# Strassen's seven products for five slabs of an MLP's first matrix product

## The chip, the cores and the metric

The kernel runs on one core of a Trainium2 chip. Its time is that of one execution on the device in microseconds; the figure for a kernel is the median of several runs. A core has a matrix engine (TensorE, "PE" in a profile, with its weight loads as "PEld"), a vector engine (VectorE, "DVE"), a scalar engine (ScalarE, "ACT"), a general engine (GpSimd, "POOL") and one that issues transfers (SyncE, "SP"). Each engine runs its own queue of instructions in order, and they wait for each other by semaphores. SBUF is the on-chip memory with 128 partitions, PSUM the memory in which TensorE sums its products.

## The reference

One layer of an encoder on 512 tokens of 1024 channels. A mixer (attention in a neighbourhood, a state-space branch, gates and an output projection w_o) is followed by a layer norm, then the channel sub-layer, which is what is edited, and a last layer norm:

```python
def sq_relu_mlp(x, w1, w2):
    return jnp.square(jax.nn.relu(x @ w1)) @ w2

h = layer_norm(DN_ALPHA * h + mix, ln1_g[l], ln1_b[l])
h = layer_norm(DN_ALPHA * h + sq_relu_mlp(h, w_ff1[l], w_ff2[l]), ln2_g[l], ln2_b[l])
```

Here x is 512 x 1024, w1 1024 x 4096 and w2 4096 x 1024, all float32.

## The kernel before

A float32 product is made from three products in a reduced-precision float form: each operand is split into a high part (a rounding copy) and a low part (the operand less the high part), and `mm3` (L402 to L406) issues high x high, low x high and high x low. The high part of weights is a copy on ScalarE (L386), the low part a subtraction on VectorE (L387). `split_weights` does both for a slab that SyncE loads (L378, buffer `ws`); the two parts go into rotating buffers (`wh`, `wl`, and a third pair `wh3`, `wl3`).

The first product of the channel sub-layer runs transposed: 32 tiles of 128 columns of w1 (the weights) against 512 tokens, stored as `h1Th` and `h1Tl` (high and low parts of the normalised tokens, channels in partitions). The tiles form four quarters `fq` of eight tiles `f`; two tiles share a slab of 256 columns `s`, 1 MB of weights, so a slab is 2 tiles x 8 blocks of 128 channels x 3 = 48 matmuls of 128 weights columns by 512 tokens. The tiles of the first two slabs of quarter 0 start ahead of the others, in halves of the tokens, before the second half's norm is done. A tile is taken out of PSUM by ScalarE, as a relu (L1672) and a square (L1678) into `r2`.

The second product, w2, uses Strassen's seven products already: `ff2_strassen` is a generator whose every step is one chunk. A chunk takes a block of w2 loaded by GpSimd's transfers (L1554, `w2r`), to which a second block is added by an accumulating transfer (L1565), splits it (L1570, L1571), and for the other operand takes differences of `r2` (L1588) and splits (`sqh`, `sql`). `into` adds the products to `acc`. The blocks rotate over three places, two of their own and one of the slab buffers `ws`. Three chunks are issued before each slab of quarter 2; quarter 3 runs the same way and is then multiplied plainly.

`acc` also holds the layer norm's result, which needs two more passes, times a row and plus a row (the "affine"): eight operations of 128 x 1024 on GpSimd (L1695), issued behind tile 4 of quarter 0. The first three w2 loads are held behind tile 0 of quarter 1 (`begin`).

The program's text gives the order only in part: a scheduler sets each engine's queue when the program is built, from dependencies and estimated durations, and buffers in pools are given out in the order of the text.

Of the kernel before, what the change touches and what calls it, by code (L numbers as in the profile page):

```python
# [19 lines left out]
P = 128  # L20
S = 512
# [336 lines left out]
def encoder_layer(ctx, tc, x, w_in, w_attn_br, w_ssd_br, w_o, w_ff1, w_ff2, pcols, rows64,  # L358
# [44 lines left out]
    def mm3(o, lh, ll, rh, rl, start, stop):  # L403
        nc.tensor.matmul(o, lh, rh, start=start, stop=False)  # L404
        nc.tensor.matmul(o, ll, rh, start=False, stop=False)  # L405
        return nc.tensor.matmul(o, lh, rl, start=False, stop=stop)  # L406
# [47 lines left out]

    def to_channels(xn, t0, nt, gcol, bcol, dsth, dstl, pool, name):

        for k in range(KD):
            tp = psx.tile([P, nt, P], F32, tag="tr", bufs=BANKS["tr"], name=f"tp_{name}_{k}")
            for t in range(nt):
                nc.tensor.transpose(tp[:, t, :], xn[t][:, k * P : (k + 1) * P], ident)  # L460
            v = pool.tile([P, nt * P], F32, tag="tc_v", bufs=2, name=f"tc_{name}_{k}")
            nc.scalar.activation(v, tp, AF.Identity, bias=pc[:, bcol + k : bcol + k + 1],
                                 scale=pc[:, gcol + k : gcol + k + 1])
# [23 lines left out]
    def bank(name, tag, shape):  # L487
        return plan.tile(name, tag, psx, shape, F32)
# [958 lines left out]
    ep = tc.tile_pool(name="ep", bufs=1, reuse_waits="tile")  # L1447
    epp = ep.__enter__()
    wo_pool = tc.tile_pool(name="wo", bufs=1, reuse_waits="tile")
    wop = wo_pool.__enter__()  # L1450
# [27 lines left out]
    for t2 in range(2):  # L1478
# [22 lines left out]
        for t in toks:  # L1501
            layer_norm_core(epp, h0[t], acc[t], f"1_{t}")
        to_channels([acc[t] for t in toks], toks[0], 2, PC_G1, PC_B1, h1Th, h1Tl, epp, f"h1_{t2}")
    wo_pool.__exit__(None, None, None)
    ep.__exit__(None, None, None)
    gp.__exit__(None, None, None)
    rx0.__exit__(None, None, None)


    ffp = ctx.enter_context(tc.tile_pool(name="ffp", bufs=1, reuse_waits="tile"))  # L1510
    NQ = D_FF // D
# [5 lines left out]
    def parts(name, shape):  # L1517

        turn["parts"] += 1
        if turn["parts"] % 3 == 0:  # L1520
            return third(w3p, name, shape)
        return [wide(wp.tile([P, 2112], F32R, tag=n, name=f"{n}_{name}"), shape[1])
                for n in ("wh", "wl")]

    def raw(name):
        turn["raw"] += 1
        pool, tag = ((ffp, "wr"), (ffp, "wr"), (wp, "ws"))[turn["raw"] % 3]
        return pool.tile([P, 4, 512], F32, tag=tag, bufs=2, name=f"w2r_{name}")
# [11 lines left out]
    def ff2_strassen(h, q0, r2):  # L1540
# [100 lines left out]
        def right1(c):  # L1641
# [4 lines left out]
            for i in range(2):  # L1646
# [7 lines left out]
                           (0, 0))  # L1654

    def ff1_tile(fq, f, last):

# [4 lines left out]
        else:  # L1662
# [8 lines left out]
        rl = ffp.tile([P, S], F32, tag="rl", bufs=2, name=f"rl{fq}_{f}")  # L1671
        nc.scalar.activation(rl, ps, AF.Relu)  # L1672
# [9 lines left out]
    def squares(name, dtype=F32):  # L1682
        return ffp.tile([P, KD, S], dtype, tag="r2", bufs=3, name=name)

    r2 = [squares(f"r2_{fq}") for fq in range(2)]
    for fq in range(2):
        for f in range(KD):
            ins = ff1_tile(fq, f, False)
            if fq == 1 and f == 0:
                begin = ins  # L1690
            if fq == 0 and f == 4:

                for t in range(NT):
                    for i, o in ((0, ALU.mult), (1, ALU.add)):
                        aff = nc.gpsimd.tensor_tensor(out=acc[t], in0=acc[t], in1=row1[i], op=o)  # L1695
                        if i == 0:
                            tc.add_manual_dep(aff.ins, ins.ins.name, mybir.DependencyInfo(
                                mybir.DependencyClass.Sync, mybir.DependencyReason.DATA),
                                reason="behind the first channels")

    r2.append(squares("r2_2"))
    run = ff2_strassen(0, 0, r2[:2])
# [17 lines left out]
    rest = ffp.tile([P, 2, 4, 512], F32R, tag="r2", bufs=3, name="w2_4")  # L1720
    slabs = [[split_weights([(w_ff2, r0 + k0 * P, i * 512, 512)], 4, 512, f"f2_3_{i}_{k0}", *x)
              for k0, x in y] for i, y in enumerate((
                  ((0, [ffp.tile([P, 4, 512], F32R, tag="wr", bufs=2, name=f"w2{n}_0") for n in "hl"]),
                   (4, [rest[:, n] for n in range(2)])),
# [85 lines left out]
```

## Time and profile before

| | |
|---|---|
| runs, median (lowest to highest) | 1183.74 us (1183.55 to 1184.21, three runs) |
| profiled execution: its span, the time by which the page's numbers go | 1182.6 us |
| TensorE busy | 1159.1 us, 98% |
| VectorE, ScalarE, GpSimd busy | 757.7, 614.7, 545.2 us |
| ten tiles of the first product (874.0 to 928.4) | 54.4 us, TensorE busy throughout |

The span is that of one execution under the profiler, the runs are timed without it. Windows of the profile are given in microseconds from the span's start. A row of a timeline has the start, the time, the engine, the line of the program, the operation, out<-in, the shape and in brackets the idle time before it with what ended it; a row of groups has minimum, median and maximum of one instruction's time in nanoseconds. The matmul's times overlap, so their cost is read from the distance of starts.

### The profile page before, as it was taken

How to read it: one execution, taken by the hardware profiler on the slowest of the kernel's cores; microseconds unless marked ns; L12 is line 12 of the kernel's file. 1: busy time of each engine (PE TensorE's matmuls, PEld its weight loads, DVE VectorE, ACT ScalarE, POOL GpSimd, SP SyncE). 2: the span in 40 equal slices, each digit the busy share in tenths (PEclk: the TensorE clock that was granted, in tenths of full speed). 3: DMA queues.
4: the chain of work that ended last, by engine and by line, in shares of the span. 5: the costliest groups of instructions: out<-in, count | busy, mean ns of one | idle time of the engine just before them, and what ended most of it. 6: DMA issues, size and time to landing. Idle time of an engine off the chain costs nothing.

```text
span 1182.6 us, 16453 instructions
## 1 busy us (share of the span) xinstructions
PE 1159.1 (98%) x6138; PEld 990.3 (84%) x6138; DVE 757.7 (64%) x1363; ACT 614.7 (52%) x1033; POOL 545.2 (46%) x588
## 2 busy tenths in 40 slices
PE   5999999999999999999999999999999999999997
PEld 5988798989888888888888888888988888878886
DVE  7757475666656656443789975556543658488856
ACT  6676573837354654423667864342253545365410
POOL 1268968777788786304567540016046121222000
PEclk9999999999999999999999999999999999999999
DMA  6353333333333331333333223544236977889511
GB/s 201 97 157 125 102 130 107 112 116 129 102 114 107 126 120 59 107 105 85 87 87 86 56 71 107 166 147 138 85 107 184 237 187 200 192 211 233 160 51 54
DMA packets 129407, 149.19 MB, mean 126 GB/s; under 512 B 22960, under 2 KB 101808, under 8 KB 129328
## 3 DMA queue, kind: packets, MB, share of 16 engines
q1 hardware_dynamic: 115696, 112.63, 31.0%
q0 software_dynamic: 13056, 34.61, 11.9%
q8 instruction: 48, 0.79, 0.3%
q10 hardware_dynamic: 576, 0.92, 0.2%
q14 instruction: 31, 0.25, 0.1%
HBM read 145.90 MB, written 2.23 MB: 125 GB/s over the span
## 4 chain that ended last, share of the span: by engine, by line
PE 86%; DMA 4%; DVE 4%; issue 2%; POOL 2%; ACT 1%; SPq 1%; DVEq 0%; POOLq 0%; ACTq 0%
PE ps_f L406 8%; PE ps_f L404 8%; PE ps_f L405 8%; PE ps_x L406 5%; PE ps_x L404 5%; PE ps_x L405 4%; PE ps_abr L1368 4%; PE ps_z L404 3%; PE ps_z L405 3%; PE ps_z L406 3%; PE ps_sbr L404 2%; PE ps_sbr L406 2%; PE ps_sbr L405 2%; PE yd L977 2%; DMA w2r<-in_w_ff 2%; PE ps_g L405 2%
## 5 line engine op out<-in xcount | busy, mean ns | idle before, releaser
L784 DVE SCALAR_TENSOR_TENSOR cv<-ps_x,pc,cv 128x511 f32<-128x511 f32 (+1 forms) x128 | 95.7, 748 | 25.6 <-ACT cv L776 22.0
L405 PE MATMUL ps_f<-h1Th,wl_f 128*128 128x512 f32 (+1 forms) x288 | 104.0, 365 | 0.0
L404 PE MATMUL ps_f<-h1Th,wh_f 128*128 128x512 f32 (+1 forms) x288 | 103.6, 365 | 0.0
L406 PE MATMUL ps_f<-h1Tl,wh_f 128*128 128x512 f32 (+1 forms) x288 | 102.0, 365 | 0.0
L1571 DVE TENSOR_TENSOR wl_f<-w2r,wh_f 128x1024 fp32r<-128x1024 f32 x42 | 50.0, 1220 | 62.5 <-ACT wh_f L1570 62.2
L404 PE MATMUL ps_z<-wh_z,hTh 128*128 128x256 f32 x256 | 75.2, 294 | 0.6 <-DVE cv L784 0.5
L406 PE MATMUL ps_z<-wl_z,hTh 128*128 128x256 f32 x256 | 71.5, 279 | 0.0
L405 PE MATMUL ps_z<-wh_z,hTl 128*128 128x256 f32 x256 | 71.5, 279 | 0.0
L1565 POOL DMA_DIRECT2D w2r<-in_w_ff x30 | 36.3, 1415 | 75.6 <-DMA w2r<-in_w_ff 49.0
L405 PE MATMUL ps_f<-wh_f,sql 128*128 128x512 f32 x168 | 65.3, 390 | 0.5 <-DVE sql L1571 0.5
L406 PE MATMUL ps_f<-wl_f,sqh 128*128 128x512 f32 x168 | 65.3, 390 | 0.1
L1570 ACT ACTIVATE wh_f<-w2r 128x1024 fp32r<-128x1024 f32 x42 | 42.6, 1052 | 43.1 <-DMA w2r<-in_w_ff 32.8
L404 PE MATMUL ps_f<-wh_f,sqh 128*128 128x512 f32 x168 | 64.9, 389 | 0.0
L1099 DVE TENSOR_TENSOR ysacc<-ps_sbr,ysacc 128x512 f32<-128x512 f32 x56 | 38.6, 690 | 39.9 <-PE ps_sbr L406 39.7
L404 PEld LDWEIGHTS ps_f<-h1Th,wh_f 128*128 128x128 f32 x288 | 53.9, 188 | 9.0 <-ACT rl L1672 0.2
L405 PEld LDWEIGHTS ps_f<-h1Th,wl_f 128*128 128x128 f32 x288 | 53.9, 188 | 8.7
L387 DVE TENSOR_TENSOR wl_f<-ws_f,wh_f 128x1024 fp32r<-128x1024 f32 x36 | 47.2, 1347 | 20.9 <-ACT wh_f L386 20.7
L406 PEld LDWEIGHTS ps_f<-h1Tl,wh_f 128*128 128x128 f32 x288 | 52.8, 188 | 8.7
L404 PE MATMUL ps_x<-hTh,wh_bc 128*128 128x512 f32 (+1 forms) x144 | 56.7, 394 | 0.0
L404 PE MATMUL ps_sbr<-yTh,wh_sbr 128*128 128x512 f32 x128 | 55.6, 434 | 0.7 <-ACT yTh L1076 0.4
L406 PE MATMUL ps_x<-hTl,wh_bc 128*128 128x512 f32 (+1 forms) x144 | 53.4, 371 | 1.7 <-DVE hTl L626 1.7
L404 PE MATMUL ps_x<-hTh,wh_x 128*128 128x512 f32 (+1 forms) x144 | 54.6, 379 | 0.0
(344 smaller groups left out, 3734.2 us busy)
## 6 DMA issues: line engine op xcount, KB each, us to landing
ws_f<-in_w_ff SPq DMA_DIRECT2D x20, 1024.0 KB
w2r<-in_w_ff POOLq DMA_DIRECT2D x18, 1024.0 KB, 7.6
bc<-acs_d SPq DMA_DIRECT2D x32, 512.0 KB
w2r<-in_w_ff POOLq DMA_DIRECT2D x30, 512.0 KB, 8.8
ws_bc<-in_w_in SPq DMA_DIRECT2D x16, 512.0 KB
ws_x<-in_w_in SPq DMA_DIRECT2D x8, 1024.0 KB
ws_z<-in_w_in SPq DMA_DIRECT2D x8, 1024.0 KB
ws_g<-in_w_in SPq DMA_DIRECT2D x8, 1024.0 KB
```

What stands on the lines that cost most here:

```text
L387: (eng[i] if isinstance(eng, tuple) else eng).tensor_tensor(out=lo[:, k], in0=st[:, k], in1=hi[:, k].bitcast(F32), op=ALU.subtract)
L404: nc.tensor.matmul(o, lh, rh, start=start, stop=False)
L405: nc.tensor.matmul(o, ll, rh, start=False, stop=False)
L406: return nc.tensor.matmul(o, lh, rl, start=False, stop=stop)
L784: op("DVE", 0.75, lambda j=j, o=o, n=n: nc.vector.scalar_tensor_tensor(out=acc()[:, o], in0=ps()[:, n], scalar=tap(j), in1=acc()[:, o], op ...
L977: nc.tensor.matmul(yd()[:, c % 2, h * HD : (h + 1) * HD], bc()[:, 1, h, :], xtok()[:, c, h * HD : (h + 1) * HD], start=True, stop=True)
L1099: op("DVE", 0.69, lambda d=d, ps=ps: nc.vector.tensor_tensor(out=ysacc[:, d, :], in0=ps(), in1=ysacc[:, d, :], op=ALU.add), r=[(ps.name, 0 ...
L1368: ins.append(nc.tensor.matmul(pss[j], u, v, start=k + p == 0, stop=k == KD - 1 and p == 2))
L1565: nc.gpsimd.dma_start(t, rows(i, n, c, k), accum_op=ALU.add)
L1570: nc.scalar.activation(hi[:, k], x, AF.Copy)
L1571: low = nc.vector.tensor_tensor(out=lo[:, k], in0=x, in1=hi[:, k].bitcast(F32), op=ALU.subtract)
```

## The change

Five slabs, slab 3 of quarter 0 and the four of quarter 1, are multiplied as a 2 x 2 product of halves: the 1024 channels in two halves of four blocks, and the slab's 256 columns in two tiles of 128; the 512 tokens are halved too. Seven products of (128 columns x 4 blocks x 256 tokens) take the place of eight: 7 x 4 x 3 = 84 matmuls of 256 tokens in place of 48 of 512.

On the token side `to_channels` keeps its float32 values (`h1a`, `h1b`), and the four sums s1 to s4 are made from them once, one on GpSimd and three on VectorE, and split. On the weight side `pair_weights` first splits three of the slab's blocks (pair "a"), then forms four differences in the slab's own buffer, two on VectorE and two on GpSimd, each in place of a block that isn't needed any more, and splits the four blocks again (pair "b"). So a slab takes two of the rotating pairs, and its buffer is held until the last low part of "b". `ff1_pair` issues the seven products into four banks of PSUM; ScalarE takes out `m1` and `m75`, VectorE adds to p26 and p43, GpSimd makes `x75` and the fourth quarter of the tile, and one relu and one square of 128 x 1024 end the slab.

Other edits go with it. The affine moves from GpSimd to VectorE, two operations behind `m75` of each of the first four slabs. `begin` becomes `m75` of slab 0 of quarter 1. The first chunk of w2 is issued ahead of the last slab's products. The buffer of `r2` is divided in two pools, sums and differences share space with buffers that are free by then, and the memory for descriptors of transfers that GpSimd issues becomes 4096 bytes.

```diff
+    s1, s2, s3, s4 = sums = [srp.tile([P, 4, 256], F32, name=f"s{i}") for i in range(4)]
+    nc.gpsimd.tensor_tensor(out=s1, in0=h1b[:, 0:4], in1=h1b[:, 4:8], op=ALU.add)
+    nc.vector.tensor_tensor(out=s3, in0=h1a[0], in1=h1b[:, 0:4], op=ALU.subtract)
+    nc.vector.tensor_tensor(out=s2, in0=s1, in1=h1a[0], op=ALU.subtract)
+    nc.vector.tensor_tensor(out=s4, in0=h1a[1], in1=s2, op=ALU.subtract)
+    for i in (2, 0, 1, 3):
+        nc.scalar.activation(sh[i], sums[i], AF.Copy)
+        nc.vector.tensor_tensor(out=sl[i], in0=sums[i], in1=sh[i].bitcast(F32), op=ALU.subtract)
...
+    def pair_weights(fq, s):
...
+        def both(hi, lo, src):
+            nc.scalar.activation(hi, src, AF.Copy)
+            nc.vector.tensor_tensor(out=lo, in0=src, in1=hi.bitcast(F32), op=ALU.subtract)
...
+        both(ah[:, 0:2], al[:, 0:2], w4[:, :, 0])
+        both(ah[:, 2], al[:, 2], b22)
+        diff(nc.vector, b11, b12, b11)
+        diff(nc.gpsimd, b12, b22, b12)
+        diff(nc.vector, b22, b22, b11)
+        diff(nc.gpsimd, b21, b21, b22)
+        both(bh[:, 0:2], bl[:, 0:2], w4[:, 0])
+        both(bh[:, 2:4], bl[:, 2:4], w4[:, 1])
+        return (ah, al), (bh, bl)
...
+    def ff1_pair(fq, s, a, b, tag="so"):
...
+        product(p1[:, 0], a, 0, plain(0, 0))
+        nc.scalar.activation(m1, p1[:, 0], AF.Copy)
+        product(p26[:, 0], a, 1, plain(0, 1))
+        product(p43[:, 1], a, 2, sums4[3])
+        product(p75[:, 1], b, 0, sums4[0])
+        product(p75[:, 0], b, 1, sums4[2])
+        ins = nc.scalar.activation(m75, p75, AF.Copy)
+        product(p26[:, 1], b, 3, sums4[1])
+        nc.vector.tensor_tensor(out=out[:, 0:4:3], in0=p26, in1=m1.unsqueeze(1).to_broadcast([P, 2, 256]),
+                                op=ALU.add)
+        nc.gpsimd.tensor_tensor(out=x75, in0=m75, in1=out[:, 3:4].to_broadcast([P, 2, 256]), op=ALU.add)
+        nc.gpsimd.tensor_tensor(out=out[:, 3], in0=x75[:, 1], in1=m75[:, 0], op=ALU.add)
+        product(p43[:, 0], b, 2, plain(1, 1))
+        nc.vector.tensor_tensor(out=out[:, 1:3], in0=p43, in1=x75, op=ALU.add)
+        flat = out.rearrange("p q t -> p (q t)")
+        nc.scalar.activation(flat, flat, AF.Relu)
+        nc.scalar.activation(flat, flat, AF.Square)
+        return ins
...
-                        aff = nc.gpsimd.tensor_tensor(out=acc[t], in0=acc[t], in1=row1[i], op=o)
...
+        aff = nc.vector.tensor_tensor(out=acc[t], in0=acc[t], in1=row1[i], op=(ALU.mult, ALU.add)[i])
...
+    for f in range(6):
+        ff1_tile(0, f, False)
+    order = [(0, 3), (1, 0), (1, 1), (1, 2), (1, 3)]
+    ready = pair_weights(*order[0])
+    run = ff2_strassen(0, 0, r2)
+    for n, (fq, s) in enumerate(order):
+        w = ready
+        if n + 1 < len(order):
+            ready = pair_weights(*order[n + 1])
+        else:
+            next(run)
+        ins = ff1_pair(fq, s, *w, "so" if n < 4 else "cb")
+        if n == 1:
+            begin = ins
+        for i in range(2) if n < 4 else ():
+            affine(n, i, ins)
...
-        for _ in range(3):
+        for _ in range(3 if f else 2):
             next(run)
```

**The order of the queues.** In the rows below `f1a_1_2` and `f1b_1_2` are the pairs "a" and "b" of slab 2 of quarter 1, `ps_f126_1_3` the bank of products 2 and 6 of slab 3, `u` holds m75 and x75, and `f2_0_3_1` is block 1 of Strassen product 3 of w2. On GpSimd's queue, from the affine to the first w2 loads, before:

```order
L1695 TENSOR_TENSOR acc3_7638<-acc3_7638,row2_7624 128x1024 [waits DVE_49,PE_49]
L1695 TENSOR_TENSOR acc0_7635<-acc0_7635,row3_7626 128x1024 [waits DMAHW4_49,Pool_49]
...
L1695 TENSOR_TENSOR acc3_7638<-acc3_7638,row3_7626 128x1024 [waits Pool_49]
L1554 DMA w2r_0_3_0_8706<-in_w_ff2 128x4x512 [waits Activation_49]
L1554 DMA w2r_0_3_1_8744<-in_w_ff2 128x4x512 [waits DMAHW4_49,DMAHW2_49,DMAHW5_49,DMAHW1_49,DMAHW6_49,DMAHW0_49,DVE_49]
...
L1565 DMA w2r_0_3_0_8706<-in_w_ff2 128x2x512 [waits DMASW0_49]
```

and in the changed program, between slabs 1 and 3 of quarter 1:

```order
L1694 TENSOR_TENSOR ws_f1_1_1_8532<-ws_f1_1_1_8532 128x4x128 [waits DMAHW5_49,DVE_49]
L1694 TENSOR_TENSOR ws_f1_1_1_8532<-ws_f1_1_1_8532 128x4x128 [waits DVE_49,Activation_49]
L1576 DMA w2r_0_3_0_8892<-in_w_ff2 128x4x512 [waits Activation_49]
L1576 DMA w2r_0_6_0_9080<-in_w_ff2 128x4x512
L1734 TENSOR_TENSOR u_1_0_8550<-u_1_0_8550,r2_1_8220 128x512 [waits DVE_49]
...
L1587 DMA w2r_0_3_0_8892<-in_w_ff2 128x2x512 [waits DMASW0_49]
...
L1694 TENSOR_TENSOR ws_f1_1_2_8650<-ws_f1_1_2_8650 128x4x128 [waits DMAHW6_49,DVE_49]
L1587 DMA w2r_0_6_0_9080<-in_w_ff2 128x2x512 [waits DMASW1_49]
...
L1576 DMA w2r_0_3_1_9033<-in_w_ff2 128x4x512 [waits DVE_49]
L1694 TENSOR_TENSOR ws_f1_1_3_8768<-ws_f1_1_3_8768 128x4x128 [waits DMAHW7_49,DVE_49]
```

The affine has gone; the w2 loads now stand between weight differences (L1694) and evictions (L1734), and an accumulating load that waits for a transfer (DMASW0) stands ahead of the differences of slab 2; the load of block 3_1 waits for VectorE.

On VectorE, the quarter's low parts up to the first w2 split, before:

```order
L387 TENSOR_TENSOR wl3_f1_1_1_8508<-ws_f1_1_1_8509,wh3_f1_1_1_8507 128x1024 [waits DMAHW5_49,PE_49,Activation_49]
...
L387 TENSOR_TENSOR wl_f1_1_2_8572<-ws_f1_1_2_8573,wh_f1_1_2_8571 128x1024 [waits DMAHW6_49,PE_49,Activation_49]
...
L1571 TENSOR_TENSOR sql_1_8196<-r2_0_8197,sqh_1_8195 128x512 [waits Pool_49]
...
L387 TENSOR_TENSOR wl_f1_1_3_8636<-ws_f1_1_3_8637,wh_f1_1_3_8635 128x1024 [waits DMAHW7_49,PE_49,Activation_49]
...
L1571 TENSOR_TENSOR wl3_f2_0_3_0_8711<-w2r_0_3_0_8706,wh3_f2_0_3_0_8710 128x1024 [waits DMASW0_49,DMASW3_49,PE_49,Activation_49]
```

and in the changed program the stretch of slab 2 of quarter 1, up to the last low part of its pair "b":

```order
L1691 TENSOR_TENSOR wl_f1a_1_2_8653<-ws_f1_1_2_8650,wh_f1a_1_2_8652 128x1024 [waits DMAHW6_49,Activation_49]
L1691 TENSOR_TENSOR wl_f1a_1_2_8653<-ws_f1_1_2_8650,wh_f1a_1_2_8652 128x512 [waits Activation_49]
L1691 TENSOR_TENSOR wl3_f1b_1_1_8537<-ws_f1_1_1_8532,wh3_f1b_1_1_8536 128x1024 [waits Activation_49]
L1737 TENSOR_TENSOR r2_1_8220<-ps_f143_1_0_8553,u_1_0_8550 128x512 [waits PE_49,Pool_49]
L1694 TENSOR_TENSOR ws_f1_1_2_8650<-ws_f1_1_2_8650 128x4x128 [waits DVE_49]
L1780 TENSOR_TENSOR acc2_7637<-acc2_7637,row2_7624 128x1024 [waits Activation_49]
L1694 TENSOR_TENSOR ws_f1_1_2_8650<-ws_f1_1_2_8650 128x4x128 [waits Pool_49]
L1732 TENSOR_TENSOR r2_1_8220<-ps_f126_1_1_8670,m1_1_1_8673 128x2x256 [waits PE_49]
L1780 TENSOR_TENSOR acc2_7637<-acc2_7637,row3_7626 128x1024 [waits DVE_49]
L1691 TENSOR_TENSOR wl_f1b_1_2_8655<-ws_f1_1_2_8650,wh_f1b_1_2_8654 128x1024 [waits Activation_49] x2
```

Where two low parts made a slab, the low parts now alternate with differences, affines (L1780) and the PSUM evictions of the slab before; the last row is the one that frees the slab's buffer.

On TensorE, the end of quarter 1's tiles and the start of the second product, before:

```order
L406 MATMUL ps_f1_1_7_8671<-h1Tl_7634,wh_f1_1_3_8635 128x512
L404 MATMUL ps_f2_0_3_0_8700<-wh3_f2_0_3_0_8710,sqh_0_8193 128x512 [waits PE_49]
...
L406 MATMUL ps_f2_0_3_0_8700<-wl3_f2_0_3_0_8711,sqh_0_8193 128x512 [waits DVE_49]
L404 MATMUL ps_f2_0_3_1_8701<-wh3_f2_0_3_0_8710,sqh_0_8193 128x512 [waits PE_49]
...
L404 MATMUL ps_f2_0_3_0_8700<-wh_f2_0_3_1_8748,sqh_1_8195 128x512 [waits Activation_49]
```

and in the changed program, in the last slab:

```order
L404 MATMUL ps_f175_1_3_8930<-sh0_8181,wh_f1b_1_3_8772 128x256 [waits Activation_49]
L404 MATMUL ps_f2_0_3_0_8886<-wh_f2_0_3_0_8896,sqh_0_8216 128x512 [waits Activation_49]
L405 MATMUL ps_f2_0_3_0_8886<-wh_f2_0_3_0_8896,sql_0_8217 128x512 [waits DVE_49]
L405 MATMUL ps_f175_1_3_8930<-sh0_8181,wl_f1b_1_3_8773 128x256 [waits DVE_49]
...
L404 MATMUL ps_f126_1_3_8928<-sh1_8182,wh_f1b_1_3_8772 128x256 [waits Activation_49]
L404 MATMUL ps_f143_1_3_8929<-h1Th_7633,wh_f1b_1_3_8772 128x256
L405 MATMUL ps_f126_1_3_8928<-sh1_8182,wl_f1b_1_3_8773 128x256 [waits DVE_49]
...
L404 MATMUL ps_f2_0_3_0_8886<-wh3_f2_0_3_1_9037,sqh_1_8218 128x512 [waits Activation_49]
L404 MATMUL ps_f2_0_3_1_8887<-wh3_f2_0_3_1_9037,sqh_1_8218 128x512
L404 MATMUL ps_f2_0_6_0_9071<-wh_f2_0_6_0_9084,sqh_0_8216 128x512 [waits Activation_49]
L404 MATMUL ps_f1_2_0_9122<-h1Th_7633,wh_f1_2_0_9114 128x512 [waits Activation_49]
```

The matmuls of w2's product 3 moved in among the last slab's, ahead of its products 6 and 4, and those for block 3_1 and product 6 follow it at once, with the first of quarter 2.

More of the change, by code (lines that the diff above doesn't have):

```diff
@@ L1526, in raw @@
         turn["raw"] += 1
-        pool, tag = ((ffp, "wr"), (ffp, "wr"), (wp, "ws"))[turn["raw"] % 3]
+        pool, tag = ((fap, "wr"), (fap, "wr"), (wp, "ws"))[turn["raw"] % 3]
         return pool.tile([P, 4, 512], F32, tag=tag, bufs=2, name=f"w2r_{name}")
@@ L1682, in squares @@
     def squares(name, dtype=F32):
[L1683 to L1699, printed above, removed]
@@ L1719, in encoder_layer @@
     r0 = (NQ - 1) * D
[L1720 removed]
+    rest = third_squares("w2_4", [P, 2, 4, 512], F32R)
     slabs = [[split_weights([(w_ff2, r0 + k0 * P, i * 512, 512)], 4, 512, f"f2_3_{i}_{k0}", *x)
               for k0, x in y] for i, y in enumerate((
[L1723 removed]
+                  ((0, [fap.tile([P, 4, 512], F32R, tag="wr", bufs=2, name=f"w2{n}_0") for n in "hl"]),
                    (4, [rest[:, n] for n in range(2)])),
```

65 lines of the change are left out of this document (56 added, 9 removed).

## The prediction

> **What bounds the kernel now.** I read the page first (busy shares, then the chain that ended last), then the waits of TensorE over the channel sub-layer, then the busy time of each engine in the stretch that is edited.
>
> ```profile
> span 1182.6 us, 16453 instructions
> PE 1159.1 (98%) x6138; PEld 990.3 (84%) x6138; DVE 757.7 (64%) x1363; ACT 614.7 (52%) x1033; POOL 545.2 (46%) x588
> PE 86%; DMA 4%; DVE 4%; issue 2%; POOL 2%; ACT 1%; SPq 1%; DVEq 0%; POOLq 0%; ACTq 0%
> PE tp_h L460 <- ACT tc_h L462: 0.5, 1, 0.5
> PE ps_f L405 <- DVE sql L1571: 0.5, 1, 0.5
> core 0: us, PE busy (x) PEld busy (x) DVE busy (x) ACT busy (x) POOL busy (x), PEclk, DMA share, GB/s
> 874.00:928.40 54.40, 54.40 (x241) 44.91 (x240) 17.85 (x12) 22.55 (x32) 32.83 (x18) 1.00 0.70 186
> 928.40:955.60 27.20, 27.20 (x122) 22.52 (x121) 19.23 (x24) 13.43 (x18) 7.92 (x8) 1.00 0.79 234
> ```
>
> TensorE is busy for 98% of the span and 86% of the last chain is its work. The two rows of waits are all that it waits between 800 us and the end. The window from 874.0 to 928.4 holds exactly the ten tiles that the change rewrites: TensorE is busy for the whole 54.40 us, at clock 1.00, VectorE for 17.85 and GpSimd for 32.83. So matmul time taken away here counts one for one, until another engine becomes the last to finish; the reserve is VectorE's idle 36 us.
>
> **What the change removes from TensorE.** Time per matmul is the spacing of starts, as they overlap:
>
> ```profile
> 900.05 0.39 PE L406 MATMUL ps_f<-h1Tl,wh_f 128*128 128x512 f32 x1
> 917.05 0.39 PE L406 MATMUL ps_f<-h1Tl,wh_f 128*128 128x512 f32 x1
> 843.16 0.28 PE L406 MATMUL ps_f<-h1Tl,wh_f 128*128 128x256 f32 x1
> 844.52 0.28 PE L406 MATMUL ps_f<-h1Tl,wh_f 128*128 128x256 f32 x1
> ```
>
> The first two rows are 25 triples apart: 17.00/75 = 0.2267 us for 512 columns. The others are four triples apart: 1.36/12 = 0.1133 us for 256, exactly half. A slab cost 48 x 0.2267 = 10.88 us; seven products of 12 are 84 x 0.1133 = 9.52. Five slabs save 5 x 1.36 = **6.8 us**, and the ten tiles become 47.6.
>
> Twice as many weight loads come with each microsecond, though those 0.1133 rows already have a new load for every matmul. The Trainium skill ("TensorE: Matmul & The Clock Gate", section "Back-to-back issue gap") gives a sustained 131 ns per matmul at 512 columns and 81 at 128, so that halves of a product pay less than half. A straight line between these is, as an estimate, 98 ns at 256, and by it a slab would go from 6.3 to 8.2 us and the five would lose 10 us. The trace has 0.2267 and 0.1133 in their place and decides against it.
>
> **What it adds elsewhere: VectorE and GpSimd.** Durations:
>
> ```profile
> 897.49 2.35 DVE L387 TENSOR_TENSOR wl_f<-ws_f,wh_f 128x1024 fp32r<-128x1024 f32 x2
> 875.53 4.73 DVE L387 TENSOR_TENSOR wl_f<-ws_f,wh_f 128x1024 fp32r<-128x1024 f32 x2 [1.97 <-ACT wh_f L386]
> L387 DVE TENSOR_TENSOR wl_f<-ws_f,wh_f x36: 1170/1218/3417, 821.6 to 1128.9; 128x1024 fp32r<-128x1024 f32 x36
> 937.75 1.29 DVE L1588 TENSOR_TENSOR as<-r 128x512 f32<-128x512 f32 x2
> L1695 POOL TENSOR_TENSOR acc<-acc,row x8: 2380/2889/3389, 873.4 to 893.9; 128x1024 f32<-128x1024 f32 x8
> L963 POOL TENSOR_TENSOR bc<-bc,amd x32: 1032/1042/1547, 70.4 to 430.0; 128x512 f32<-128x512 f32 x32
> L918 POOL TENSOR_TENSOR xw<-xtok,wst x16: 609/615/617, 72.8 to 455.0; 128x256 f32<-128x256 f32 x16
> L1099 DVE TENSOR_TENSOR ysacc<-ps_sbr,ysacc x56: 676/692/693, 179.4 to 502.5; 128x512 f32<-128x512 f32 x56
> L1624 DVE TENSOR_TENSOR acc<-acc,ps_f x40: 677/680/686, 960.4 to 1131.3; 128x512 f32<-128x512 f32 x40
> ```
>
> Two VectorE operations of 1024 take 2.35 us when GpSimd computes nothing, so 2.35 - 1.22 = 1.14 from start to start; two of 512 give 1.29 - 0.68 = 0.61. The same pair took 4.73 us while GpSimd's affine (L1695) ran, and one reached 3.417; the affine in turn goes from 2.380 to 3.389. They take turns: the time of one is added to the other's. VectorE's reads of PSUM with one operand in SBUF (L1099, L1624) spread by 17 ns only, so I let them run beside GpSimd. GpSimd takes 1.04 for 512 and 0.61 for 256.
>
> The Trainium skill ("SBUF — State Buffer", section "Who interferes with whom") states that turn-taking: of a VectorE instruction with two SBUF inputs and a GpSimd one that reads SBUF, the second to issue blocks until the first is done. The trace agrees, with 4.73 against 2.35. Were the ports shared freely, the sum below would hold VectorE's time alone, and would stall nothing.
>
> Per slab the new code gives VectorE three low parts of 1024 and one of 512 (L1691), two differences of 512 (L1694), two affines of 1024 (L1780, in the first four slabs) and two PSUM evictions (L1732, L1737). By turns that is 5 x 1.14 + 3 x 0.61 = 7.53, and GpSimd adds two differences, one 512 and one 256 eviction: 3 x 1.04 + 0.61 = 3.73. Together **11.3 us against TensorE's 9.52** in a slab with affines, 9.0 in the fifth. The evictions' 2 x 0.68 lies beside GpSimd, or adds 1.4. ScalarE has 3.5 thousand elements per partition of copies, 0.77 of evictions and two passes of 1024; at 2.00 us for two of 1024 (row below) some 6.5 us, under 9.5. It is no bound by itself.
>
> **The sum, place by place.**
>
> ```profile
> 859.43 0.56 ACT L462 ACTIVATE tc_h<-tp_h,pc 128x256 f32<-128x256 f32 x1 [0.72 <-PE tp_h L460]
> 873.95 0.60 ACT L1672 ACTIVATE rl<-ps_f 128x512 f32<-128x512 f32 x1 [0.60 <-PE ps_f L406]
> 874.45 2.00 ACT L386 ACTIVATE wh_f<-ws_f 128x1024 fp32r<-128x1024 f32 x2
> 993.08 0.76 POOL L1554 DMA_DIRECT2D w2r<-in_w_ff  x1 [15.52 <-DVE wl_f L387]
> 998.89 2.45 POOL L1565 DMA_DIRECT2D w2r<-in_w_ff  x2 [5.05 <-DMA w2r<-in_w_ff]
> w2r<-in_w_ff POOLq DMA_DIRECT2D x30, 512.0 KB, 8.8
> ```
>
> The token sums begin when ScalarE has written the last channels, 859.43 + 0.56 = 860.0; GpSimd's s0 takes 2.4 (L1695's least), so VectorE starts s1 at about 862.5. From there to the last low part of slab (1,3) its queue holds 31 operations of 1024 and 17 of 512, 45.7 us, and GpSimd 14 of 1.04 and 4 of 0.61-0.65, 17.1: 925.3 at the earliest. TensorE, never stalled, wants that low part after 398 half matmuls and the 24 full ones of W2 that stand ahead of it: 874.0 + 45.1 + 5.4 = 924.5. That alone is a stall of **0.8 us**; with the eight evictions in series (5.4) 6.2.
>
> The later place is the start of the second product. Its second block (w2r 3_1) is loaded into the slab buffer of slab (1,2), which is free when VectorE has made that slab's last low part. Up to there stand 23 operations of 1024 and 12 of 512 on VectorE, and on GpSimd eight differences, three evictions of 512 and three of 256: 26.2 + 7.3 + 13.3 = 46.8, so 909.3 (912.7 with five PSUM evictions in series). Then come the load, 998.89 - 993.08 = 5.8; the accumulating pair, 0.7 for the second issue and 8.8 to land; a copy on ScalarE, 1.0; and behind it in ScalarE's order a square (1.0), an eviction (0.6), two copies of 512 (1.2), two of 1024 (2.0) and one of 512 (0.6), which is split by VectorE (0.7): **22.4 us**, or 23.7 if the difference and eviction ahead of the pair on GpSimd (1.04 each) aren't done while the load flies. TensorE wants the block after all five slabs, 24 + 5 full matmuls later: 874.0 + 47.6 + 6.6 = 928.2. So 909.3 + 22.4 = 931.7 is a stall of 3.5; with 23.7 it is 4.8; with the evictions in series and 1 us of other transfers it is 912.7 + 23.7 + 1 = 937.4, or 9.2. I take **4.1**, between the first two, as the PSUM rows speak for evictions that run beside GpSimd. The stalls are one: what TensorE loses at the first place it needn't wait for at the second.
>
> Costed at nothing: the kept channels (they replace a rotating buffer; ScalarE waited there for TensorE, 859.43); the affine's leaving GpSimd (its 22.8 us lay beside TensorE's work, and its price on VectorE is in the 11.3). An accumulating W2 load waits in GpSimd's queue for the load before it and stands ahead of a weight difference: if that load lands late, the difference, its high and low copies and TensorE are late by as much. The smaller ring of descriptors for GpSimd's transfers: three issues took 2.55 us (below) with no wait in them, which bounds it at 0 to 0.85 us an issue; I take 0.
>
> ```profile
> 873.43 22.81 POOL L1695 TENSOR_TENSOR acc<-acc,row 128x1024 f32<-128x1024 f32 x8 [53.38 <-ACT r L1678]
> 896.19 2.55 POOL L1554 DMA_DIRECT2D w2r<-in_w_ff  x3
> ```
>
> After 955 us the loop of loads, splits and matmuls is released by TensorE's own progress, so what is gained before is carried to the end. **Net -6.8 + 4.1 = -2.7**: a profiled span of 1179.9 and, the median of the runs standing 1.1 above the span (1183.74 against 1182.6), **1181.0 us**. What a measurement of this kernel tells from no change is about 0.2%, 2.4 us, that is 1181.4 to 1186.1.
>
> **Rivals.**
> (a) VectorE and GpSimd bind, and the start of W2 waits for them: evictions in series, transfers slow, stall 9.2, net +2.4, **1186.2**. For: the 11.3 against 9.52 in four slabs and ScalarE's strict order. Against: VectorE ahead of the stage is idle, and the PSUM rows. It ends slower once the stall passes 6.8 + 2.4; a long contended stretch (the window from 928.4 has DMA at 0.79) can carry it to 1189.
> (b) The same at half weight: stall 5 to 8, net -1.8 to +1.2, **1183** and no change.
> (c) Nothing stalls; the full 6.8, **1176.9**. For: VectorE is idle for 36 of the window's 54 us now. Against: the port sum, which is over TensorE's time by 1.8 in each of four slabs.
> (d) The saving isn't there since weight loads of 0.19 us bind at 256 columns: 84 x 0.19 = 15.9 a slab, +25. The 0.1133 spacing excludes it; under 0.01.
>
> **How the numbers follow.** The forecast, a stall of 1 to 4.4 (1178.0 to 1181.3), and (c) make faster: 0.40 + 0.08. (b) has 0.33. (a), with what lies beyond it, 0.19. The likeliest one's own range is 1178.0 to 1181.4. The range to hold 8 in 10 leaves out half of (c) below and the far part of (a): 1177.2 to 1186.8.
>
> **What would show it.** In the changed profile ten tiles' matmuls at 0.113 spacing; TensorE's waits on VectorE's low parts (L1691) and on the first W2 splits (L1593) near 915 to 935, together 3 to 5 us; VectorE nearly full from 862 to 925, with L1691 stretched above 1.2 where GpSimd's L1694 runs; w2r 3_1 issued near 909. If TensorE's waits are under 1 us, (c) holds; if over 8, (a). Waits in another place, such as the transposes or the evictions' banks, would make the steps above wrong.

## The result, and the profile after

The changed kernel takes 1205.51 us (median of four runs, 1204.04 to 1207.05) against 1183.97 for the kernel before beside it: a ratio of 1.0179, 95% interval 1.0165 to 1.0194. It is slower by 21.5 us, where 2.7 us less were forecast.

The page of the changed kernel:

```profile
span 1203.7 us, 16894 instructions
PE 1163.6 (97%) x6318; PEld 999.3 (83%) x6318; DVE 811.3 (67%) x1408; ACT 628.7 (52%) x1047; POOL 555.0 (46%) x601
```

TensorE's waits from 860 to 960 us (total, how often, the longest):

```profile
PE ps_f L405 <- DVE wl_f1b L1691: 9.7, 3, 4.6
PE ps_f L405 <- DVE sql L1593: 2.8, 1, 2.8
PE ps_f L404 <- ACT wh_f1a L1690: 1.5, 1, 1.5
```

Three windows (length; busy time and instructions of TensorE, its weight loads, VectorE, ScalarE and GpSimd; granted clock, share of the transfer engines, GB/s), and in the last row one of the kernel before:

```profile
910.00:920.00 10.00, 5.64 (x33) 5.24 (x31) 6.95 (x4) 1.06 (x1) 4.87 (x4) 0.83 1.08 242
920.00:930.00 10.00, 8.05 (x62) 7.44 (x61) 8.52 (x8) 8.22 (x11) 6.00 (x5) 1.00 0.20 77
930.00:940.00 10.00, 5.83 (x25) 5.71 (x26) 10.00 (x9) 5.19 (x6) 3.84 (x4) 0.66 0.73 122
...
900.00:920.00 20.00, 20.00 (x89) 16.39 (x89) 2.45 (x3) 7.13 (x10) 8.08 (x7) 1.00 1.08 282
```

TensorE waits for 14 us, not 4, and for 12.5 of them where the prediction looked: for the low parts of pair "b" and for the first w2 splits. Two things in the windows weren't in the prediction at all. From 910 to 920 no engine is busy for more than 7 of 10 us while the transfers run at 1.08. They ran at 1.08 in the kernel before too, from 900 to 920, and TensorE was busy throughout: what is new isn't the traffic but what stands behind it. TensorE's first wait in this window is for VectorE; ScalarE from 912 and VectorE from 917 on are idle until a slab's weights arrive. And the granted clock, 1.00 before in every window from 860 to 960, falls to 0.83 and 0.66.

Adding up the distance of the starts of TensorE's matmuls from 874.9 to 986.0 gives the account. The 420 half matmuls (256 columns) and 167 full ones (512) of the stretch would take 85.5 us at 0.1133 and 0.2267; they took 25.4 more. Of that 16.0 us are seven gaps of 0.4 to 4.9 us; 6.5 are matmuls at about half the pace behind gaps; 2.8 are half matmuls that run at 0.120 in place of 0.1133. Set against the 6.8 that the products save, that is +18.6; another 1.4 come from three small waits near 1036 to 1065, and 0.9 was there when the stretch began (1.1 at 790 us already, ahead of the sub-layer that is edited). Together 20.9 of the spans' difference of 21.1.

**The first gap, at 910.** The timeline of VectorE and ScalarE ahead of it, TensorE last:

```profile
894.11 0.69 DVE L1694 TENSOR_TENSOR ws_f<-ws_f 128x512 f32<-128x512 f32 x1 [1.41 <-POOL ws_f L1694]
907.23 1.39 DVE L1780 TENSOR_TENSOR acc<-acc,row 128x1024 f32<-128x1024 f32 x1 [1.07 <-ACT u L1730]
909.75 3.80 DVE L1780 TENSOR_TENSOR acc<-acc,row 128x1024 f32<-128x1024 f32 x1
913.47 2.87 DVE L1691 TENSOR_TENSOR wl_f1b<-ws_f,wh_f1b 128x1024 fp32r<-128x1024 f32 x2
911.27 1.06 ACT L1690 ACTIVATE wh_f1b<-ws_f 128x1024 fp32r<-128x1024 f32 x1 [1.91 <-POOL ws_f L1694]
915.27 0.39 PE L405 MATMUL ps_f<-sh,wl_f1b 128*128 128x256 f32 x1 [4.36 <-DVE wl_f1b L1691]
```

Two groups of instructions by line (minimum, median and maximum in ns):

```profile
L1694 POOL TENSOR_TENSOR ws_f<-ws_f x10: 1287/1498/2215, 871.9 to 931.3; 128x512 f32<-128x512 f32 x10
L1737 DVE TENSOR_TENSOR r<-ps_f,u x5: 676/677/679, 891.4 to 952.7; 128x512 f32<-128x512 f32 x5
```

The affine at 909.75 takes 3.80 us, as three GpSimd operations run beside it, and the low part that TensorE wants stands behind it. A difference takes GpSimd 1.29 to 2.2 us, not 1.04. The PSUM evictions (L1737) keep their 0.68, as the prediction took them. What the sum of turns left out is the hand-over: VectorE waits for GpSimd's differences or for ScalarE's copies and evictions (1.41 and 1.07 us in the first two rows; with four more such waits from 873 on, 5.8 us in all).

**The second and third, at 919.7 and 929.** The timeline of ScalarE, SyncE's issue of slab (1,3), GpSimd's issues of w2's accumulating transfers around it, and TensorE:

```profile
920.39 1.58 ACT L1690 ACTIVATE wh_f1a<-ws_f 128x1024 fp32r<-128x1024 f32 x2 [8.06 <-DMA ws_f<-in_w_ff]
904.99 0.37 SPq L1681 DMA_DIRECT2D ws_f<-in_w_ff  x1
902.06 2.50 POOL L1587 DMA_DIRECT2D w2r<-in_w_ff  x2 [1.05 <-DMA w2r<-in_w_ff]
907.50 2.43 POOL L1587 DMA_DIRECT2D w2r<-in_w_ff  x2
934.17 0.58 PE L405 MATMUL ps_f<-sh,wl_f1b 128*128 128x256 f32 x1 [4.63 <-DVE wl_f1b L1691]
```

The same issue in the kernel before:

```profile
880.29 0.37 SPq L378 DMA_DIRECT2D ws_f<-in_w_ff  x1
```

The buffer that this slab is loaded into holds slab (1,1) until the last low part of its pair "b", at 904.96, since the differences are made in it. So the load is issued 25 us later than before. W2's first two loads have landed by then, but the four accumulating transfers of the rows above are under way beside it, and it arrives 15.4 us after its issue. ScalarE waits for it in order, then VectorE, and TensorE has no pair for slab (1,3). From 921.5 to 934.1 VectorE works without a pause, two affines and two w2 splits among its work, so the gap at 929 has both causes: the late slab and the turns.

### The profile page after: what moved, and what is told of

It reads as the page before. It is cut to its first block, busy times and chain, and to the rows that moved or that the text cites. A ratio compares the mean times of both kernels' runs of the same rounds, so it can differ in the third digit from the quotient of the medians.

```text
span 1203.7 us, 16894 instructions
## 1 busy us (share of the span) xinstructions
PE 1163.6 (97%) x6318; PEld 999.3 (83%) x6318; DVE 811.3 (67%) x1408; ACT 628.7 (52%) x1047; POOL 555.0 (46%) x601
## 5 line engine op out<-in xcount | busy, mean ns | idle before, releaser
L404 PE MATMUL ps_f<-h1Th,wh_f 128*128 128x512 f32 (+1 forms) x208 | 73.0, 357 | 0.4 <-ACT wh_f L386 0.4
L405 PE MATMUL ps_f<-h1Th,wl_f 128*128 128x512 f32 (+1 forms) x208 | 73.1, 356 | 0.0
L406 PE MATMUL ps_f<-h1Tl,wh_f 128*128 128x512 f32 (+1 forms) x208 | 70.8, 356 | 0.0
L1587 POOL DMA_DIRECT2D w2r<-in_w_ff x30 | 36.5, 1424 | 54.7 <-DMA w2r<-in_w_ff 33.6
L1576 POOL DMA_DIRECT2D w2r<-in_w_ff x18 | 16.3, 905 | 82.6 <-DVE wl_f L1593 58.3
L1414 POOL TENSOR_TENSOR gt<-gt,ysacc 128x512 f32<-128x512 f32 x8 | 12.0, 1504 | 91.4 <-ACT gt L1117 90.1
L405 PE MATMUL ps_x<-hTh,wl_bc 128*128 128x512 f32 (+1 forms) x144 | 52.7, 366 | 0.0
L406 PE MATMUL ps_x<-hTl,wh_x 128*128 128x512 f32 (+1 forms) x144 | 52.5, 365 | 0.0
```

The source lines that it names most:

```text
L1414: gy = nc.gpsimd.tensor_tensor(out=g1, in0=g1, in1=ysacc[:, d, :], op=ALU.mult)
L1576: load = nc.gpsimd.dma_start(t, rows(i, n, c))
L1587: nc.gpsimd.dma_start(t, rows(i, n, c, k), accum_op=ALU.add)
```

## The experiments

Two theories: **turn-taking** (VectorE and GpSimd, with affines and differences, are later than TensorE) and **transfer** (the slab's load, held back by the buffer, collides with w2's transfers). Beside them stood two smaller terms, the half pace behind gaps and the 0.120 us.

**Without the affines.**

```diff
-        for i in range(2) if n < 4 else ():
-            affine(n, i, ins)
```

> The eight affines of the layer norm (multiplication by a row, addition of a row, VectorE L1780) are left out, so the sum that enters the last norm lacks them; all else as in the changed kernel. Turn-taking theory (VectorE and GpSimd together need 11.3 us a slab against TensorE's 10): four slabs lose 2.3 us of VectorE each, the gap of 4.5 us at 910 goes, and those behind it shrink by as much; 1189 to 1193. Transfer theory (the load of slab (1,3), issued at 905 behind four w2 transfers, lands at 920): its buffer comes free 2 to 4 us sooner but the load still shares the queues with w2; the gap at 910 goes, the later ones stay; 1196 to 1200.

Measured: 1194.72 us, ratio 1.0098 (1.0082 to 1.0115), 11 us less than the changed kernel. The gap at 910 is gone, and the gaps of the stretch add up to 10.1 us in place of 16.0. The time lies between the two expectations, and the run doesn't part the theories. ScalarE's row for slab (1,3):

```profile
908.68 1.58 ACT L1690 ACTIVATE wh_f1a<-ws_f 128x1024 fp32r<-128x1024 f32 x2
```

With 9 us of VectorE's time back the buffer is free earlier. The load is issued at 901.8, ahead of w2's accumulating transfers (903.5 and 906.4), and is taken up 6.9 us later without a wait. So leaving out the affines took away the late load as well. Of the remaining gaps 2.4 us are at 916 and 921, the others at the start of w2 (932 to 942).

**W2's loads later.**

```diff
-        if n == 1:
+        if n == 2:
             begin = ins
```

> The first w2 loads are held behind m75 of slab (1,1) in place of slab (1,0), some 12 us later, so that the load of slab (1,3) is issued ahead of them. Transfer theory: ScalarE's wait for that slab (8.06 us idle up to 920.4) goes, the gaps at 920 and 929 (1.65 and 5 us) shrink to 1 or 2, and only the start of w2 waits a little more; 1196 to 1200. Turn-taking theory: the gap of 4.5 at 910 stays, and w2 starts later with nothing won; 1204 to 1210.

Measured: 1201.52 us, 1.0148 (1.0133 to 1.0163). The rows of ScalarE:

```profile
911.63 1.58 ACT L1690 ACTIVATE wh_f1a<-ws_f 128x1024 fp32r<-128x1024 f32 x2 [2.56 <-DMA ws_f<-in_w_ff]
945.54 2.00 ACT L386 ACTIVATE wh_f<-ws_f 128x1024 fp32r<-128x1024 f32 x2 [3.10 <-DMA ws_f<-in_w_ff]
```

Slab (1,3) is there at 911.6, 5.6 us after its issue at 906.0, as the transfer theory says. But the collision was only handed on: the next slab, (2,0), issued at 935.4 among w2's loads, arrives at 945.5, and TensorE waits 6.0 us for it. So the gain was 4 us, just short of what was expected.

**Three slabs, two, and a load held back.** Three and two slabs shorten the list; the others become plain tiles:

```diff
-    order = [(0, 3), (1, 0), (1, 1), (1, 2), (1, 3)]
+    order = [(0, 3), (1, 0), (1, 1)]
```

> Only slabs (0,3), (1,0) and (1,1) are made by Strassen's products; (1,2) and (1,3) are plain tiles, their affines stay on VectorE, and the first w2 chunk is issued behind the last tile. Both theories: the plain slabs need 2.3 us of VectorE each in 10.9 us, so the turns have room and the slab buffers come free early; no gap above 2 us in the stage. Three slabs at the 0.120 us that the changed kernel's matmuls take save 3 x 0.8 = 2.4; 1181 to 1186. If the token sums or the move of the affine cost by themselves, over 1188.

Measured: 1195.62 us, 1.0103 (1.0086 to 1.012). Both theories had it at 1181 to 1186, so both were short here. ScalarE and TensorE in that run:

```profile
920.85 2.00 ACT L386 ACTIVATE wh_f<-ws_f 128x1024 fp32r<-128x1024 f32 x2 [13.08 <-DMA ws_f<-in_w_ff]
...
925.27 0.79 PE L404 MATMUL ps_f<-h1Th,wh_f 128*128 128x512 f32 x1 [9.45 <-ACT rl L1759]
925.87 0.63 PE L405 MATMUL ps_f<-h1Th,wl_f 128*128 128x512 f32 x1
926.29 0.63 PE L406 MATMUL ps_f<-h1Tl,wh_f 128*128 128x512 f32 x1
```

There is one gap, of 9.5 us, and it is the transfer's: the plain slab (1,3) takes the buffer of the Strassen slab (1,1) all the same, its load is issued at 902.9 and lands at 920.85. ScalarE waits for it with the relu of an earlier tile behind the copy, TensorE waits for that bank. My expectation had the buffers free early, wrongly. Behind the gap the matmuls are 0.43 apart, at the clock's half.

> Only slabs (0,3) and (1,0) are made by Strassen's products; the three others of quarter 1 are plain. Transfer theory: plain slabs give their buffers back once they are split, so the load of (1,3) is issued near 888, ahead of w2's first load near 895, and no wait of TensorE above 1 us is left in the stage; two slabs save 2 x 0.8 us at 0.120 us a matmul: 1181 to 1184. If the token sums or the affine on VectorE cost by themselves, 1186 or more.

Measured with `order = [(0, 3), (1, 0)]`: 1183.18 us, ratio 0.9998 (0.9988 to 1.0008), no change. Now (1,1) is plain, its buffer is free early, (1,3) is issued at 890.65, ahead of w2's first load at 892.55, and this row is TensorE's whole list of waits from 800 us on:

```profile
PE tp_h L460 <- ACT h1b L462: 0.4, 1, 0.4
```

So the sums, pairs and moved affines of two slabs let TensorE wait nowhere when the load isn't late. The 1.6 us that two slabs should save at 0.120 us a matmul (below) don't show in the medians (by their interval, from 1.4 us less to 0.9 more); what takes them isn't shown. The late load by itself, in the kernel before:

```diff
+            if fq == 1 and f == 2:
+                held = ins
+            if fq == 1 and f == 6:
+                tc.add_manual_dep(split_weights.load.ins, held.ins.name, ...
```

> The kernel before, with one edit: the load of slab (1,3) may start only behind the square of tile 2 of quarter 1, near 902 in place of 880. No Strassen product, no sum, no difference. Transfer theory: it lands near 918, as it shares the queues with w2; ScalarE waits for it ahead of the relu of tile 4, TensorE for a bank: a gap of 4 to 9 us, and matmuls at half rate behind it: 1188 to 1196. Turn-taking theory: a load takes 5.6 us and TensorE wants the slab at 917.5, so nothing is lost: 1183 to 1185.

Measured: 1187.95 us, 1.0031 (1.0019 to 1.0043), 4.5 us slower by a later load alone. In its profile ScalarE takes the slab up at 917.72, behind w2 copies that here stand ahead of it, and TensorE's gap is 1.5 us: less than expected, as this order put the wait behind the relu of the tile before. The direction is the transfer theory's. Of the 3.8 us between this profile and that of the kernel before, 1.5 are at the gap and 0.75 come near 1016; the other 1.5 are there already at 790 us, ahead of the edit, where the profiles of this document lie from 1.5 us ahead of to 2.4 behind that of the kernel before. So the late load cost about 2.2 us by the traces, and 2.2 to 5.1 by the medians' interval: it costs time alone, but a small part of the 21.5.

**All on VectorE.** The differences and small evictions leave GpSimd:

```diff
-        diff(nc.gpsimd, b12, b22, b12)
+        diff(nc.vector, b12, b22, b12)
...
-        nc.gpsimd.tensor_tensor(out=x75, in0=m75, ...
+        nc.vector.tensor_tensor(out=x75, in0=m75, ...
```

> All five slabs, but the weight differences and the two small evictions run on VectorE, not on GpSimd; the same results. Turn-taking theory: these operations took VectorE's turn on GpSimd as well, and there they take 1.0 to 1.3 us, on VectorE 0.6, so a slab needs 11.1 in place of 11.3 and the hand-overs: 1199 to 1206. If the engines ran side by side, VectorE's load would rise from 8.9 to 11.1 us in each slab: 1209 to 1214.

Measured: 1198.84 us, 1.0128 (1.0113 to 1.0144), nearly 7 us better than the changed kernel with the same work on one engine less. GpSimd's help was none: it took VectorE's turn, with slower operations and hand-overs. The gap at 910 shrinks to 1.5 us. What stays is the transfer, on ScalarE:

```profile
917.00 1.58 ACT L1690 ACTIVATE wh_f1a<-ws_f 128x1024 fp32r<-128x1024 f32 x2 [11.56 <-DMA ws_f<-in_w_ff]
```

And the group of the low parts of "b":

```profile
L1691 DVE TENSOR_TENSOR wl_f1b<-ws_f,wh_f1b x10: 1211/1218/1227, 872.6 to 935.3; 128x1024 fp32r<-128x1024 f32 x10
```

The ten low parts of "b" now take 1.21 to 1.23 us, where the changed kernel has up to 3.16.

**Fewer bytes.**

```diff
-            for t, k in zip(x, halves):
+            for t, k in zip(x, halves) if h else ():
                 nc.gpsimd.dma_start(t, rows(i, n, c, k), accum_op=ALU.add)
```

> The changed kernel without the accumulating transfers of the first w2 stage, so that its blocks lack their second summand: half the bytes of w2 there. Transfer theory: the load of slab (1,3), issued near 905, lands 5 to 9 us earlier than 920, the gaps at 920 and 929 shrink and so do the waits for w2's blocks, and only the 4.5 us of turn-taking at 910 with its slow clock and the slower 256s are left: 1188 to 1196. Turn-taking theory, with transfers of no account: 1202 to 1206.

Measured: 1193.93 us, 1.0078 (1.0062 to 1.0094), 11.6 less than the changed kernel with every computing instruction still there. The load of (1,3), issued at 905.1 as in the changed kernel, is taken up by ScalarE at 910.54, 5.4 us later in place of 15.4. The gaps of the stretch fall from 16.0 to 10.0 us and the slow clock's share from 6.5 to 4.2. Not all of the 11.6 is the slab's, as these transfers were waited for at the start of w2 too. And the first gap, which was expected to stay at 4.5 us, shrank to 1.8, with one of 0.8 ahead of it for slab (1,3), as the affine there took 2.00 us in place of 3.80:

```profile
909.83 2.00 DVE L1780 TENSOR_TENSOR acc<-acc,row 128x1024 f32<-128x1024 f32 x1
```

GpSimd's queue lacks the issues of these transfers here; whether that is why the affine's turn came out shorter isn't shown.

**The pace of the half matmuls.** The kernel before with its ten tiles in token halves:

```diff
+            if fq == 1 or fq == 0 and s == 3:
+                ff1_half(w1, j, ps, 0)
+                ff1_half(w1, j, ps, 1)
```

> The kernel before, but the ten tiles are computed in two token halves, so 96 matmuls of 256 columns take the place of 48 of 512 in a slab; the work on all other engines is that of the kernel before. At the predicted 0.1133 us nothing changes, 1183 to 1185. At the 0.120 us of the changed kernel's rows 10 x 48 x 0.0067 = 3.2 us more: 1186 to 1188. Were each weight load of 0.19 us unhidden, 480 x 0.075 = 36 us more.

Measured: 1186.86 us, 1.0026 (1.0017 to 1.0036). TensorE without a gap, 48 matmuls apart:

```profile
879.75 0.28 PE L404 MATMUL ps_f<-h1Th,wh_f 128*128 128x256 f32 x1
885.50 0.28 PE L404 MATMUL ps_f<-h1Th,wh_f 128*128 128x256 f32 x1
```

5.75/48 = 0.1198 us. So a slab of 84 costs 10.06 and saves 0.82, not 1.36: five save 4.1. The rows that the prediction read, at 843, belong to the first two slabs, whose weights are stored 64 bytes further (a shift of 16 words). All rotating buffers were moved by that, the third pair likewise:

```diff
-        return [wide(wp.tile([P, 2112], F32R, tag=n, name=f"{n}_{name}"), shape[1])
+        return [wide(wp.tile([P, 2112], F32R, tag=n, name=f"{n}_{name}"), shape[1], 16)
```

> As the run with ten tiles in token halves, but all rotating weight buffers begin 64 bytes later, as those of the first two slabs do, whose matmuls of 256 ran at 0.113 us. Theory that the address decides the pace (weights and moving operand begin at the same place modulo 128 bytes at 0.120, 64 bytes apart at 0.113): rows at 0.113, 1183 to 1185, the 3 us are back. If the pace of a long series of 256s is 0.120 wherever its operands lie: 1186 to 1188.

Measured: 1191.2 us, 1.006 (1.0044 to 1.0076), slower still. The halves gained a little, the matmuls of 512 lost more; two of them in that run, 48 matmuls apart:

```profile
999.74 0.40 PE L406 MATMUL ps_f<-wl_f,sqh 128*128 128x512 f32 x1
1010.94 0.40 PE L406 MATMUL ps_f<-h1Tl,wh_f 128*128 128x512 f32 x1
```

11.20/48 = 0.2333 us in place of 0.2267. With the ten tiles' own buffers moved alone, the shift being an argument of `parts`:

```diff
-                                        *parts(f"f1_{fq}_{s}", [P, KD, 256]))
+                                        *parts(f"f1_{fq}_{s}", [P, KD, 256], 16 if fq == 1 or fq == 0 and s == 3 else 0))
```

> The kernel before with the ten tiles in token halves, only their own weight buffers 64 bytes later. Address theory: the 3.2 us of the halves are gone and those of the shifted 512s as well: 1183 to 1185. If long series of 256s run at 0.120 wherever they lie: 1186 to 1188.

Measured: 1185.71 us, 1.0012 (1.0002 to 1.0022). The 512s are at 0.2267 again, the halves at 0.118. So the place of the weights in memory moves both paces, but 64 bytes bring the halves only from 0.120 to 0.118. The 0.1133 did come in two runs, with three and with five Strassen slabs and all buffers moved (rows below), and not with two slabs and the same shift; what else it needs stays open.

**Versions that might be faster.** These join edits shown above. Two slabs, all on VectorE, every buffer 64 bytes later:

```diff
-    order = [(0, 3), (1, 0), (1, 1), (1, 2), (1, 3)]
+    order = [(0, 3), (1, 0)]
...
-        diff(nc.gpsimd, b12, b22, b12)
+        diff(nc.vector, b12, b22, b12)
```

> Two slabs by Strassen's products, (0,3) and (1,0), with the differences and small evictions on VectorE and the weight buffers 64 bytes later. Address theory: 2 x 1.36 = 2.7 us saved, 1180 to 1182. If the address does nothing: 1181.5 to 1184, as with two slabs before.

1187.12 us, 1.0027 (1.0015 to 1.0038): no waits, but the halves are at 0.118 and the 512s at their slower pace. Three slabs, (1,1) and (1,3) plain, else the same:

```diff
+    pairs_at = ((0, 3), (1, 0), (1, 2))
...
+        if at in pairs_at:
+            w = ready if n < 2 else pair_weights(*at)
...
+        else:
+            ff1_tile(1, 2 * at[1], False)
+            ins = ff1_tile(1, 2 * at[1] + 1, False)
```

> Three slabs by Strassen's products, (0,3), (1,0) and (1,2), with (1,1) and (1,3) plain, all on VectorE, weight buffers 64 bytes later. Transfer theory: the load of (1,3) takes the buffer of the plain (1,1), which is free near 890, so it is issued ahead of most of w2's loads and no gap as with the first three slabs (9.8 us) comes: 1179 to 1184. If the number of Strassen slabs decides and not the buffer's hold: 1190 to 1196 as with three slabs in a row.

TensorE's rows, and its waits from 800 us on:

```profile
875.77 0.28 PE L405 MATMUL ps_f<-sh,wl_f1a 128*128 128x256 f32 x1
881.21 0.28 PE L404 MATMUL ps_f<-h1Th,wh_f1a 128*128 128x256 f32 x1
```

```profile
PE ps_f L404 <- DVE r L1737: 3.6, 1, 3.6
```

1192.74 us, 1.0071 (1.0053 to 1.0089). The time is in the range that was given to the rival, but not for its reason: the 9.5 us gap is gone, as the transfer theory has it, and the halves are at 5.44/48 = 0.1133. But the last Strassen eviction is now late for w2's first operands (3.6 us, with 2.9 of slow clock behind it), and the 512s lose about 5.8. All five slabs of the changed kernel with the shift, on VectorE:

```diff
-        diff(nc.gpsimd, b21, b21, b22)
+        diff(nc.vector, b21, b21, b22)
...
-        return [wide(wp.tile([P, 2112], F32R, tag=n, name=f"{n}_{name}"), shape[1])
+        return [wide(wp.tile([P, 2112], F32R, tag=n, name=f"{n}_{name}"), shape[1], 16)
```

> All five slabs, all on VectorE, weight buffers 64 bytes later. Transfer theory: the load of (1,3) still waits for the buffer of (1,1) to 902 and lands near 917; faster matmuls only lengthen the wait: 1196 to 1200, as without the shift (1198.8). If the pace of the matmuls carried through: 1195 to 1196.5.

TensorE's rows in slab (1,0), 48 matmuls apart:

```profile
879.76 0.28 PE L405 MATMUL ps_f<-h1Th,wl_f1a 128*128 128x256 f32 x1
885.20 0.28 PE L406 MATMUL ps_f<-h1Tl,wh_f1a 128*128 128x256 f32 x1
```

1200.79 us, 1.0143 (1.0121 to 1.0165), above what was expected. The halves have the predicted pace here, 5.44/48 = 0.1133, and the time is no shorter than the 1198.84 of the same program without the shift: the wait for (1,3) is 5.5 us, and the 512s lose 4.7. Two slabs, on VectorE, with only their own pairs moved:

```diff
-            "p (b k c) -> p b k c", b=4, k=4) for t in parts(f"f1{x}_{fq}_{s}", [P, KD, 256])]
+            "p (b k c) -> p b k c", b=4, k=4) for t in parts(f"f1{x}_{fq}_{s}", [P, KD, 256], 16)]
```

> Two slabs by Strassen's products, (0,3) and (1,0), all on VectorE; only their weight pairs begin 64 bytes later, every buffer whose matmuls have 512 columns stays where it is. Address theory: the two slabs run at 0.113 and the 512s at 0.2267 again, 2 x 1.36 = 2.7 us saved: 1180.5 to 1182 if the kernel before stands at 1183.4 to 1184. If the shift's loss was not the 512s': 1184 or more.

1182.47 us, 0.9992 (0.9983 to 1.0002). The pairs ran at 0.118, not 0.113, and one wait of 0.6 us came back. Nothing tried is faster than the kernel before beyond doubt.

## Why the prediction was wrong, step by step

The step that failed is the stall: 4.1 us, from a sum of turns alone. In its place came gaps of 16.0 us and 6.5 of slow clock behind them, from turns that ended 7 us later than summed and from a slab's load that the prediction didn't follow.

- **What bounds the kernel, and that time taken from TensorE counts**: right, and with it the ground for the loss. A stage that TensorE fills has no room for a wait.
- **The saving, 6.8 us**: mis-sized. The spacing was read from 13 rows at 843 and taken for any matmul of 256 columns; in the changed slabs, and in the kernel before with halves, it is 0.120, and 4.1 us are saved. The estimate by the Trainium skill ("TensorE: Matmul & The Clock Gate", section "Back-to-back issue gap"), a loss of 10 us, isn't borne out either: of that two slabs would have 4, and without waits they lost at most 0.9 by the interval.
- **Turns of VectorE and GpSimd, 11.3 against 9.52 us**: the mechanism was right and the PSUM evictions lie beside GpSimd as said, but the stall was sized at 0.8 us at one place, the last slab. The first stall came a slab earlier, 4.5 us at 910, at the low part of "b" of (1,2). The prediction had this slab's last low part end at 909.3, which would have been in time for TensorE's arrival at 910.6, and didn't ask what a later end would do there; it ended at 916.3. The sum began 1.2 us early (the token sum that it starts with began at 863.75, not 862.5), left out 5.8 us of hand-overs and took 1.04 us for a GpSimd operation that takes 1.29 at least.
- **The start of w2, 3.5 to 9.2 us**: the block 3_1 was issued at 916.65, not 909.3, since it waits for the same late low part; the waits of 2.8, 0.4 and 0.3 us at that place are the smaller part. The prediction's second sum for this place, 23.7 us, should be 24.5 by its own rows (22.4 and two operations of 1.04), which changes little.
- **What is costed at nothing**: the term that failed outright isn't even in the list. The prediction named the buffer that w2's block takes, and not that slab (1,3) takes such a buffer too. Its load moved from 880.3 to 905.0, in among w2's accumulating transfers, and took 15.4 us where 5.4 were enough without them. Holding a buffer longer moved the load that follows into another's traffic. What the prediction feared in that list, a difference on GpSimd held up by a late w2 load, didn't come: no difference there waited for a transfer.
- **The clock**: no row before showed a drop, and none was reckoned with; 6.5 us.
- **Rival (a)** had the side and part of the mechanism; its stall of 9.2 us stands against gaps of 16.0 with 6.5 of slow clock, and its far end, 1189, is 16 us short. Rivals (c) and (d) are out.
- **The affine's move, the smaller ring**: the affine's price is real (11 us less without it, the late load's part among them). Undoing the ring alone wasn't tried; with the small ring in place two slabs ran without a wait, and w2's first load landed 6.0 us after its issue there (5.7 in the kernel before), so nothing points to it.

How the 21.5 us divide isn't shown. Without affines 11 go, without GpSimd's part 7, without the accumulating bytes 12; these overlap, since each lateness sets the next, and each longer gap brings its slow clock.

## What to carry to other kernels

When an edit makes a buffer live longer, follow the buffer to the load that comes next into it: when is it issued then, and what else is on the transfer engines at that time? Sum an engine's turns with the hand-overs between engines that work in place on the same data, and compare the sum with the bound engine's arrival at every place, not at the last one. A gain of half a percent from fewer products is smaller than one gap and its slow clock.

## What was not expected of the hardware

**Half pace behind a gap.** In all these profiles a gap of TensorE up to 2.1 us that stood alone had no more than three slow matmuls behind it, and gaps of 2.4 us or more had them for 3 to 6 us: the 512s 0.427 apart, the 256s 0.212. Gaps close together count as one: 0.8 and 1.8 us within 4 us, in the run without accumulating transfers, had 16 slow matmuls behind them. The rows behind the gap at 910.6 are

```profile
916.35 0.41 PE L406 MATMUL ps_f<-sl,wh_f1b 128*128 128x256 f32 x1
916.56 0.41 PE L404 MATMUL ps_f<-sh,wh_f1b 128*128 128x256 f32 x1
916.78 0.41 PE L405 MATMUL ps_f<-sh,wl_f1b 128*128 128x256 f32 x1
```

so the gap of 4.5 us at 910.6 cost 6.0, and one of 2.9 at 949.6 cost 4.5. The granted clock of the windows agrees (0.57 and 0.50 in the two halves of 920 to 930 in the run with three slabs). The Trainium skill ("TensorE: Matmul & The Clock Gate", section "Part 1: The HAM clock gate (the "warmup" mystery)") says that the clock goes to half after an idle window of about 3.4 us and comes back after about as much work; the runs agree roughly with the second (3 to 6 us), and show the drop from 2.4 us of idling on.

**The pace depends on where the weights lie.** Moving weight buffers by 64 bytes, with no other edit, changed matmuls of 256 columns from 0.120 to 0.118 us (ten tiles in halves) or to 0.113 (five slabs on VectorE), and those of 512 from 0.2267 to 0.2333 in the rows above. Which of the two paces the halves take isn't explained by any run here.
